# Second stick-breaking heads' queries and keys, and a third block of new rows, turned by DMA transposes

## The chip, the core and the metric

The kernel runs on one core of a Trainium2 chip. The metric is device time in microseconds (us) of one execution, lower is better. The engines of the core have queues of their own and run in order: TensorE (PE, with its weight loads as PEld), VectorE (DVE), ScalarE (ACT), GpSimd (POOL) and SyncE (SP), which here only issues DMAs.

## The reference, cut to what matters

One layer of a streaming encoder, 256 tokens, width 2048, all in float32. Eight "fox" heads (softmax attention with a forget bias) and eight stick-breaking heads, each 128 wide, stand side by side; a gated feed-forward network with a short convolution follows.

```
def stick_breaking_attention(q, k, v):
    scale = HEAD_DIM ** -0.5
        z = jnp.einsum('bhqd,bhkd->bhqk', qi.astype(jnp.float32), k32) * scale
        mask = k_pos[None, :] < q_pos[:, None]
        log_beta = jax.nn.log_sigmoid(z)
        log_one_minus = jnp.where(mask, log_beta - z, 0.0)
        suffix = lax.cumsum(log_one_minus, axis=key_axis, reverse=True) - log_one_minus
        weights = jnp.where(mask, jnp.exp(log_beta + suffix), 0.0)
        return jnp.einsum('bhqk,bhkd->bhqd', weights.astype(v.dtype), v)
...
        h = rms_norm(x, attn_norm[layer])
        x = x + hybrid_mixer(h, w_in[layer], ..., w_out[layer])
        h = rms_norm(x, ffn_norm[layer])
        x = x + conv_ffn(h, w_up[layer], conv_w[layer], conv_b[layer], w_down[layer])
```

## The kernel before

All weights are streamed once. A step loads 128x2048 float32 of weights by SP (`load`, L266; five buffers `w_raw`), ScalarE rounds them to `w_hi` (L276) and VectorE subtracts to get the rest, `w_lo` (L284); three products of high and low parts make one float32 product on PE. The Python loop at L1431 writes out the order of every engine by hand: in iteration n it emits the loads of step n+6, the cast and subtraction of step n+2, the matmuls of step n, what follows step n-1, and one or two "ticks" that move the attention heads on by a stage each (`tick`, L245). Each engine then works through its own list in that order.

Steps come in this order: the values of the fox heads, then "units" (L545) for rows rA and rB (queries and keys of the fox heads 0 to 3 and 4 to 7), rC (queries and keys of the stick-breaking heads 0 to 3), vB (their values), rD (queries and keys of stick-breaking heads 4 to 7), then the output projection, then the feed-forward network. The steps of the output projection are called W0 to W18 here. W0 to W10 take the fox heads: by `ORDER` (L1096) W1 and W3 make `acc_o` of the columns 2 (`out_rows(0, 2, ...)`), W5 and W9 those of columns 3, and the rest are products of `out_unit`, on the tiles `bank_a`, `bank_bc`, `bank_b`. W11 to W18 take the stick-breaking heads. W15 to W18 finish the columns c = 2 and c = 3, which are blocks 2 and 3 of the new rows.

A stick-breaking head (`sb_head`, L832) goes through: scores `ps_z` on PE (L840, L841), mask added by VectorE (L844), three activations of ScalarE on `e` (L847 to L849) and one VectorE operation on it (L850), high and low parts `sps` (L854, L855), sums with a triangular matrix on PE (L859, L861), weights `w` and their high and low parts `ws` (L864, L867 on ScalarE, L868 on VectorE), output `ps_o` on PE (L759, L761), eviction to `oSb`. Here the heads are numbered 0 to 7.

Queries and keys come out of a unit with tokens on partitions and must be turned so that the head's width is on partitions. For the fox heads and for rD this is done by PE (`to_heads`, L675: 16 transposes `ps_h` for rD, then four ScalarE evictions, the queries' with the scale 1/sqrt(128)). For rC it is done by DMA (`turned_heads`, L659): `send_turned` (L642) copies each 128x512 block to a tile `room`, its two 16-bit halves apart, the first block by ScalarE and the second by VectorE, and issues a DMA transpose on SP for each; three ticks later `take_turned` (L653) copies the halves back together. The scale of these queries is one VectorE operation (L672).

`heads_tile` (L350) has two buffers, which its callers take in turn: qB0, kB0, then kB1, qB1, so that kB1 stands where qB0 stood.

New rows x2 (tile `xb`) of 512 columns c are turned likewise for the feed-forward network: blocks c = 0 and 1 by DMA (`turned_rows`, L1002, then `split_turned`, L1017), c = 2 and 3 by PE (`next_rows`, L997: eight transposes `ps_x` each). The high and low parts go to `hT`. The first step of the feed-forward network reads blocks 0 and 1, its second step first block 2, then block 3 (L1229).

Of the kernel before, what the change touches and what calls it, by code (L numbers as in the profile page):

```python
# [9 lines left out]
F32 = mybir.dt.float32  # L10
# [6 lines left out]
P = 128  # L17
# [30 lines left out]
def hybrid_layer(  # L48
# [67 lines left out]
    rstd1 = const.tile([P, NT], F32, name="rstd1")  # L116
    headR = const.tile([P, NH], F32R, name="headR")
    nrstd1 = const.tile([P, NT], F32, name="nrstd1")
    hT = big.tile([P, KT, 2, S], F32R, name="hT")
    xp = xf.rearrange("(t p) d -> p t d", p=P)  # L120

# [416 lines left out]
    def of_sums(q):  # L538
        n, t = q
        return lambda i, p, _: sums_cell[1][:, p, n, i, t * P : (t + 1) * P]  # L540
# [1 line left out]
    def of_raw(kb, t):  # L542
        return lambda i, p, _: of_half(hT[:, 4 * kb + i], p, t)

    def unit(c_first, c_second, dst, done):  # L545

        cols = (c_first, c_second)
        w11, w12, w21, w22 = (rows_of(wi, 4 * h, 4, cols[n], 512) for h in range(2) for n in range(2))
        mem, bank = {}, {}
        slots = dict(zip("acbe", (0, 1, 2, 3) if turn[0] else (2, 3, 0, 1)))  # L550
        turn[0] ^= 1

        def r(t, negative=False):
            return (nrstd1 if negative else rstd1)[:, t : t + 1]

        def product(name, new, lhs, weights, load_=(), sums=None, plus=None, follow=None):
            parts = []

            def loads():
                for key, src in load_:  # L560
                    mem[key] = load(src)
                if plus is not None:
                    nc.gpsimd.dma_start(
                        mem[weights].rearrange("p (a b) -> p a b", a=4), plus, accum_op=ALU.add
                    )

            def prepare():
                parts.extend(split(mem[weights], 4, 512))

            def matmuls():  # L570
                if new:
                    bank[name] = bank_tile(f"bank_{name}", slots[name])
                in_three([bank[name]], parts, 4, lhs, new, True)

            new_step(loads, sums, prepare, matmuls, follow)

        def plain(n, kq, order, follow=None):
            def matmuls(parts):
# [12 lines left out]
        def sum_of(other):  # L591
            return lambda: dve.tensor_tensor(mem["11"], mem["11"], mem[other], op=ALU.add) and None

        out = {}

        def evict(name, n, t, negative=False):
            def follow():
                if not out:
                    out.update(dst())
                act.activation(out[n, t], bank[name], AF.Identity, scale=r(t, negative))  # L600
                yield

            return follow

        def add(name, n, t, negative=False):
            dve.scalar_tensor_tensor(
                out[n, t], bank[name], r(t, negative), out[n, t], op0=ALU.mult, op1=ALU.add
            )

        def then_add(*what):  # L610
            def follow():
                yield
                for w in what:
                    add(*w)

            return follow

        def finish():
            act.activation(out[0, 1], bank["a"], AF.Identity, scale=r(1))
            yield  # L620
            add("c", 0, 0)
            others.append(done(out))

        product("a", True, of_raw(0, 0), "11", [("11", w11)], follow=evict("a", 0, 0))
        product("c", True, of_raw(1, 0), "21", [("21", w21)])
        product("b", True, of_sums(T5), "11", [("12", w12)], sum_of("12"), follow=evict("b", 1, 1))
        plain(1, 0, [(1, "e"), (0, "b")])
        product("a", False, of_sums(S2), "11", [("22", w22)], sum_of("22"), follow=evict("a", 1, 0, True))
        plain(1, 1, [(1, "e"), (0, "b")], then_add(("e", 1, 1)))
        product("a", False, of_sums(T7), "12", plus=w22, follow=then_add(("a", 1, 1, True)))  # L630
        product("b", False, of_sums(S4), "22", follow=then_add(("b", 1, 0)))
        plain(0, 0, [(0, "c"), (1, "a")])
        product("a", False, of_raw(1, 1), "11", plus=w21)
        plain(0, 1, [(1, "a"), (0, "c")], finish)
# [4 lines left out]

        return make  # L640

    def send_turned(rows, room):  # L642
        planes = room.bitcast(U16).rearrange("p h s -> p (h s)").rearrange("p (t c) -> p t c", t=NT)
        for t, (move, (source, words)) in enumerate(zip((act.copy, dve.tensor_copy), rows)):
            move(
                planes[:, t].rearrange("p (b f) -> p b f", b=2),
                source.bitcast(U16).rearrange("p (f b) -> p b f", b=2),
            )
            nc.sync.dma_start_transpose(
                words.bitcast(U16).rearrange("p (g s) -> p g s", s=P), planes[:, t]  # L650
            )

    def take_turned(move, words, t, room):  # L653
        move(
            room.bitcast(U16).rearrange("p h (s b) -> p b h s", b=2)[:, :, :, t * P : (t + 1) * P],
            words.bitcast(U16).rearrange("p (b h s) -> p b h s", b=2, h=4),
        )

    def turned_heads(rows):  # L659
        for n, key in enumerate(("qB0", "kB0")):  # L660
            tile_of[key] = heads_tile(key)
            send_turned([(rows[n, t], rows[n, t]) for t in range(NT)], tile_of[key])
            yield
        yield
        yield
        yield
        for t in range(NT):
            take_turned(act.copy, rows[0, t], t, tile_of["qB0"])
        yield
        for t in range(NT):  # L670
            take_turned(dve.tensor_copy, rows[1, t], t, tile_of["kB0"])
        dve.tensor_scalar(tile_of["qB0"], tile_of["qB0"], QSCALE, None, op0=ALU.mult)  # L672
        yield

    def to_heads(rows, keys, scales):  # L675

# [12 lines left out]
    def fox_rows(half):  # L689
        def done(rows):  # L690
# [20 lines left out]
            yield from to_heads(rows, (f"qA{half}", f"kA{half}"), (gq, g_k))  # L711
            for h in range(4 * half, 4 * half + 4):
                waiting.append(fox_head(h, half))

        return done

    def sb_rows(half):
        def done(rows):
            if half:
                while started["sb"] < 4:  # L720
                    yield
                yield
                yield
                yield from to_heads(rows, ("qB1", "kB1"), (QSCALE, 1.0))
            else:
                while started["fox"] < NH:
                    yield
                yield from turned_heads(rows)
            ready.add(f"qB{half}")
            if "vB" in ready:  # L730
                start_sb(half)

        return done

# [156 lines left out]

    unit(0, WF, row_tiles("rA", 0), fox_rows(0))
    unit(512, WF + 512, row_tiles("rB", 1), fox_rows(1))
    unit(B0, B0 + WF, row_tiles("rC", 0), sb_rows(0))
    unit(B0 + 2 * WF, B0 + 2 * WF + 512, value_rows, values_done)
    D_UNIT = len(steps)
    unit(B0 + 512, B0 + WF + 512, row_tiles("rD", 0), sb_rows(1))
    W_OUT = len(steps)


# [99 lines left out]
        yield  # L1000

    def turned_rows(c):  # L1002
        if c == 0:
            room = heads_tile("xT0")
            w = at.tile([P, NT, 512], F32, name="xw0", tag="v0")
            words = [w[:, t] for t in range(NT)]
        else:
            room = at.tile([P, 4, S], F32, name="xT1", tag="v1")
            words = [rows_tile(f"xw1{t}", 1) for t in range(NT)]
        send_turned([(x2[:, t, c * 512 : (c + 1) * 512], words[t]) for t in range(NT)], room)  # L1010
        yield
        for t, move in enumerate((act.copy, dve.tensor_copy)):
            take_turned(move, words[t], t, room)
        following.append(split_turned(c, room))
        yield

    def split_turned(c, room):  # L1017
# [24 lines left out]
    def out_rows(group, c, kh):  # L1042
# [22 lines left out]
        def follow():  # L1065
# [8 lines left out]
            while group == 0 and held:  # L1074
                held.pop()()
            if group == 1:
                after.append(turned_rows(c) if c < 2 else next_rows(c))
                yield
                if c == 0:
                    spare.append(heads_tile("spare").rearrange("p a b -> p (a b)")[:, :512])  # L1080
# [319 lines left out]
    def factors1():  # L1400
        yield from token_factors(rstd1, ss1)
        dve.tensor_scalar(nrstd1, rstd1, -1.0, None, op0=ALU.mult)

    def head_parameters():
        columns(pcol, prow, 50)
# [95 lines left out]
```

## Time and profile before

| what | us |
|---|---|
| median of 3 runs (lowest, highest) | 1091.05 (1090.68, 1091.85) |
| the profiled execution, its own time | 1090.48 |
| its span, first to last instruction | 1088.7 |
| largest idle of ScalarE in the stretch of the change, before L915 | 4.47 |

The page cuts the span into 40 slices of 27.2 us; a digit is the busy share in tenths. ScalarE and VectorE read:

```profile
DVE  5988899889897877779978988889888889789996
ACT  6767797778766857667667777667667667677762
```

Counted from 0, the change lies in slices 10 to 14 (272 to 408 us). VectorE is close to full in slice 11 and has room in slice 12 and after; ScalarE has more room in slices 12 to 14. An average over a slice tells nothing of the order in which operations wait for each other, so the lists of instructions in order of time are needed.

### The profile page before, as it was taken

Reading aid. Unit: us, or ns where it says so; the run is one execution under the profiler, and the core shown is the slowest. Engines: PE = TensorE matmul, PEld = TensorE weight load, DVE = VectorE, ACT = ScalarE, POOL = GpSimd, SP = SyncE. Lnnn points to the kernel's source line nnn. Section 1 sums busy time; section 2 is a strip of 40 time slices with the busy share of each in tenths; the row PEclk is TensorE's granted clock in tenths of the full one; section 3 lists DMA queues with packets and bytes.
Section 4 is the critical chain, followed back from the end, with each engine's and each line's share of the span. In section 5 each row is a group of like instructions: output and inputs, shape, how many; then the busy total and the mean of one; then the engine's idle time right before and its main releaser. Section 6 shows DMA issues by size and latency. Waiting matters only on the chain.

```text
span 1088.7 us, 14642 instructions
## 1 busy us (share of the span) xinstructions
PE 1083.8 (100%) x5669; PEld 935.6 (86%) x5669; DVE 929.5 (85%) x927; ACT 761.5 (70%) x972; POOL 59.8 (5%) x53
## 2 busy tenths in 40 slices
PE   9999999999999999999999999999999999999998
PEld 9988888888888888888888888888888888888887
DVE  5988899889897877779978988889888889789996
ACT  6767797778766857667667777667667667677762
POOL 0000000001000000000000000100000000000000
PEclk9999999999999999999999999999999999999999
DMA  8897986989777765669899598996969699896995
GB/s 311 271 273 240 276 199 208 231 244 281 236 219 239 191 202 189 198 173 257 266 228 309 168 260 270 250 292 172 309 191 287 228 245 270 222 311 167 285 267 140
DMA packets 183663, 260.62 MB, mean 239 GB/s; under 512 B 13080, under 2 KB 106666, under 8 KB 183594
## 3 DMA queue, kind: packets, MB, share of 16 engines
q1 hardware_dynamic: 160138, 212.36, 57.9%
q0 software_dynamic: 23280, 47.19, 24.7%
q8 instruction: 44, 0.72, 0.3%
q14 instruction: 25, 0.20, 0.1%
q10 hardware_dynamic: 176, 0.14, 0.0%
HBM read 255.48 MB, written 2.10 MB: 237 GB/s over the span
## 4 chain that ended last, share of the span: by engine, by line
PE 100%; DVE 0%; issue 0%
PE pu L1235 45%; PE bank_a L304 18%; PE bank_b L304 11%; PE bank_c L304 6%; PE acc_o L304 6%; PE acc_v L424 4%; PE bank_e L304 3%; PE acc L304 2%; PE ps_x L194 1%; PE ps_o L759 1%; PE ps_h L683 0%; PE ps_z L840 0%; PE ps_o L761 0%; PE ps_i L188 0%; PE half L304 0%; PE ps_z L859 0%
## 5 line engine op out<-in xcount | busy, mean ns | idle before, releaser
L284 DVE TENSOR_TENSOR w_lo<-w_raw,w_hi 128x2048 fp32r<-128x2048 f32 (+2 forms) x251 | 555.8, 2218 | 120.4 <-ACT w_hi L276 119.4
L276 ACT CAST w_hi<-w_raw 128x2048 fp32r<-128x2048 f32 (+2 forms) x251 | 464.4, 1854 | 213.8 <-PE pu L1235 86.4
L1235 PE MATMUL pu<-hT,w_hi 128*128 128x512 f32 x1408 | 333.5, 389 | 0.0
L1235 PEld LDWEIGHTS pu<-hT,w_hi 128*128 128x128 f32 x1408 | 263.0, 188 | 53.7
L1235 PEld LDWEIGHTS pu<-hT,w_lo 128*128 128x128 f32 x1408 | 180.0, 191 | 6.6
L1235 PE MATMUL pu<-hT,w_lo 128*128 128x256 f32 x1408 | 182.0, 283 | 0.0
L1288 POOL DMA_DIRECT2D w_raw<-in_w_down_dram x31 | 39.8, 1302 | 712.9 <-DVE w_lo L284 386.9
L1160 ACT ACTIVATE tap<-up,ccol 128x256 f32<-128x256 f32 x176 | 74.6, 495 | 0.0
L304 PE MATMUL bank_a<-w_hi,hT 128*128 128x512 f32 x192 | 48.6, 395 | 0.0
L304 PEld LDWEIGHTS bank_a<-w_hi,hT 128*128 128x128 f32 x192 | 35.2, 188 | 6.8
L304 PE MATMUL bank_a<-w_hi,s 128*128 128x512 f32 x160 | 40.0, 392 | 0.0
L304 PE MATMUL bank_b<-w_hi,s 128*128 128x512 f32 x160 | 40.0, 392 | 0.0
L304 PE MATMUL bank_a<-w_hi,g 128*128 128x512 f32 x152 | 38.0, 392 | 0.0
L424 PE MATMUL acc_v<-w_hi,hT 128*128 128x344 f32 x192 | 35.7, 327 | 0.0
L304 PEld LDWEIGHTS bank_b<-w_hi,s 128*128 128x128 f32 x160 | 28.9, 189 | 5.3
L304 PEld LDWEIGHTS bank_a<-w_hi,s 128*128 128x128 f32 x160 | 28.9, 189 | 5.2
L1165 DVE TENSOR_TENSOR gate<-gate,tap 128x512 f32<-128x512 f32 x44 | 30.3, 689 | 2.3
L1165 DVE TENSOR_TENSOR val<-val,tap 128x512 f32<-128x512 f32 x44 | 30.3, 688 | 2.3
L1146 DVE TENSOR_TENSOR up<-t,R 128x512 f32<-128x512 f32 x44 | 30.5, 692 | 1.5
L304 PE MATMUL acc_o<-w_hi,oSb 128*128 128x512 f32 x128 | 31.7, 396 | 0.0
L1153 ACT ACTIVATE gate<-up,ccol 128x256 f32<-128x256 f32 x44 | 24.1, 594 | 10.8 <-DVE up L1146 5.4
L304 PEld LDWEIGHTS bank_a<-w_hi,g 128*128 128x128 f32 x152 | 27.4, 189 | 4.9
(304 smaller groups left out, 1420.1 us busy)
## 6 DMA issues: line engine op xcount, KB each, us to landing
w_raw<-in_w_up_dram SPq DMA_DIRECT2D x88, 1024.0 KB, 7.1
w_raw<-in_w_down_dram SPq DMA_DIRECT2D x44, 1024.0 KB, 6.9
w_raw<-in_w_in_dram SPq DMA_DIRECT2D x40, 1024.0 KB, 6.9
w_raw<-in_w_down_dram POOLq DMA_DIRECT2D x31, 1024.0 KB, 9.9
w_raw<-in_w_out_dram SPq DMA_DIRECT2D x16, 1024.0 KB, 6.5
w_raw<-in_w_in_dram POOLq DMA_DIRECT2D x10, 1024.0 KB, 9.8
w_raw<-in_w_in_dram SPq DMA_DIRECT2D x13, 516.0 KB, 5.1
xb<-in_x_dram POOLq DMA_DIRECT2D x4, 512.0 KB, 9.2
```

The lines of the kernel that those rows point to most:

```text
L194: nc.tensor.transpose(ps[:, j, t * P : (t + 1) * P], x2[:, t, (k + j) * P : (k + j + 1) * P], ident)
L276: copy(hi[:, :n], raw[:, :n])
L284: dve.tensor_tensor(lo[:, :n], raw[:, :n], f32(hi[:, :n]), op=ALU.subtract)
L304: nc.tensor.matmul(o, lhs(i, l, t), r[:, i, :] if cut is None else r[:, i, cut], start=starts and j == 0, stop=stops and j == 3 * n - 1, s ...
L424: nc.tensor.matmul(banks[j][t][:, :VC], of_half(hT[:, k], l, t), w[:, 0, m * VC : (m + 1) * VC], start=k == l == 0 and w is mem["parts", i ...
L759: mm(po, v, w[:, i, :S], start=m == 0, stop=False)
L1146: dve.tensor_tensor(u[:, :, 2:], t2, R, op=ALU.mult)
L1153: act.activation(a[:, j, :], u[:, j, 2:], AF.Identity, scale=ccol[:, 2, f : f + 1], bias=ccol[:, 3, f : f + 1],)
L1160: act.activation(taps[w][:, j, :], u[:, j, w : w + S], AF.Copy, scale=ccol[:, w, f : f + 1])
L1165: dve.tensor_tensor(a, a, tap, op=ALU.add)
L1235: nc.tensor.matmul(acc[:, j, S:] if low else acc[:, j, :], (lo if low else hi)[:, i, j * P : (j + 1) * P], hT[:, k, 0, :] if low else hT[: ...
L1288: nc.gpsimd.dma_start(mem[weights].rearrange("p (a b) -> p a b", a=4), plus, accum_op=ALU.add)
```

## The change

Unit rD's keys are sent by DMA as soon as head 3 has issued its scores (`second_keys`), and its queries when the unit is finished (`second_heads`); both are copied out and in by ScalarE alone. The start of the heads 4 to 7 is no longer behind `to_heads`. The queries' scale goes into the factors of the units rC and rD (`rstdq`), so L672 and the scale of the eviction go. Block c = 2 of the new rows is turned by DMA, and its split into high and low parts follows the take at once, in the same iteration, instead of with the next two iterations.

```
+    rstdq = const.tile([P, NT], F32, name="rstdq")
...
-    def unit(c_first, c_second, dst, done):
+    def unit(c_first, c_second, dst, done, factors=rstd1, keys=None):
...
+            return (nrstd1 if negative else rstd1 if n else factors)[:, t : t + 1]
...
-        product("b", False, of_sums(S4), "22", follow=then_add(("b", 1, 0)))
+        product("b", False, of_sums(S4), "22", follow=then_add(("b", 1, 0), then=keys))
...
+    def take_turned(words, room, moves=BOTH):
+        for t, (move, word) in enumerate(zip(moves, words)):
+            move(
+                room.bitcast(U16).rearrange("p h (s b) -> p b h s", b=2)[:, :, :, t * P : (t + 1) * P],
+                word.bitcast(U16).rearrange("p (b h s) -> p b h s", b=2, h=4),
+            )
...
+    def second_keys(rows):
+        while started["sb"] < 4:
+            yield
+        send_heads(rows, 1, "kB1", (act.copy, act.copy))
+        yield
+        yield
+        yield
+        take_heads(rows, 1, "kB1", act.copy)
+
+    def second_heads(rows):
+        send_heads(rows, 0, "qB1", (act.copy, act.copy))
+        yield
+        yield
+        yield
+        take_heads(rows, 0, "qB1", act.copy)
+        start_sb_when("qB1")
...
-    unit(B0 + 512, B0 + WF + 512, row_tiles("rD", 0), sb_rows(1))
+    unit(B0 + 512, B0 + WF + 512, row_tiles("rD", 0), second_heads, rstdq, second_keys)
...
+            room = at.tile([P, 4, S], F32, name="xT2", tag="v0")
+            words = [tmp.tile([P, 6 * P], F32, name=f"xw2{t}", tag="sps")[:, :512] for t in range(NT)]
         send_turned([(x2[:, t, c * 512 : (c + 1) * 512], words[t]) for t in range(NT)], room)
         yield
-        for t, move in enumerate((act.copy, dve.tensor_copy)):
-            take_turned(move, words[t], t, room)
-        following.append(split_turned(c, room))
+        take_turned(words, room)
+        if c == 2:
+            for _ in split_turned(c, room):
+                pass
+        else:
+            following.append(split_turned(c, room))
...
-                after.append(turned_rows(c) if c < 2 else next_rows(c))
+                after.append(turned_rows(c) if c < 3 else next_rows(c))
```

Three places show how the lists move. The first is ScalarE's list between head 2 and head 3. Before, behind head 2's weights and parts (the last row is the cast for W0):

```order
L864 ACTIVATE w<-ps_z 128x384
L867 CAST ws<-w 128x256
L854 CAST sps<-e 128x384
L974 CAST hT<-oFox 128x4x256
L276 CAST w_hi<-w_raw 128x2048
```

Now the two copies of the keys stand ahead of these casts:

```order
L880 ACTIVATE w<-ps_z 128x384
L883 CAST ws<-w 128x256
L870 CAST sps<-e 128x384
L650 COPY kB_2547<-rD_2281 128x1024
L650 COPY kB_2547<-rD_2282 128x1024
L990 CAST hT<-oFox 128x4x256
L277 CAST w_hi<-w_raw 128x2048
```

Further on in the same list, before, from the unit's last eviction (rD) over the casts for W2 and W3 to head 3's `w`:

```order
L619 ACTIVATE rD_2279<-bank_a,rstd_91 128x512
L276 CAST w_hi<-w_raw 128x2048 x2
L884 ACTIVATE oSb_2681<-ps_o,pcol 128x256
L768 ACTIVATE osq<-ps_o 128x256
L915 CAST hT<-oFox 128x2048
L864 ACTIVATE w<-ps_z 128x384
```

Now, with the takes of the keys ahead and the copies of the queries between the casts for W2 and W3:

```order
L660 COPY kB_2547<-rD_2281 128x2x4x128
L660 COPY kB_2547<-rD_2282 128x2x4x128
L622 ACTIVATE rD_2280<-bank_a,rstdq 128x512
L277 CAST w_hi<-w_raw 128x2048
L650 COPY qB_2667<-rD_2279 128x1024
L650 COPY qB_2667<-rD_2280 128x1024
L277 CAST w_hi<-w_raw 128x2048
L900 ACTIVATE oSb_2694<-ps_o,pcol 128x256
L784 ACTIVATE osq<-ps_o 128x256
L931 CAST hT<-oFox 128x2048
L880 ACTIVATE w<-ps_z 128x384
```

Six copies have come into this stretch, two of them (the takes of the queries) behind the last row shown.

The second place is VectorE's list at head 4's mask, before:

```order
L844 TENSOR_TENSOR ps_z<-ps_z,masksR 128x2x128
L1071 SCALAR_TENSOR_TENSOR xb<-acc_o_2667,rg_125,xb 128x512
L1071 SCALAR_TENSOR_TENSOR xb<-acc_o_2668,rg_125,xb 128x512
L284 TENSOR_TENSOR w_lo<-w_raw,w_hi 128x2048 x2
L850 SCALAR_TENSOR_TENSOR e<-ps_z,e 128x384
```

and now, where the operation on `e` stands right behind the mask (at head 5 too), and the rows' update and W5's and W6's subtractions behind it:

```order
L860 TENSOR_TENSOR ps_z<-ps_z,masksR 128x2x128
L866 SCALAR_TENSOR_TENSOR e<-ps_z,e 128x384
L1093 SCALAR_TENSOR_TENSOR xb<-acc_o_2680,rg_126,xb 128x512
L1093 SCALAR_TENSOR_TENSOR xb<-acc_o_2681,rg_126,xb 128x512
L285 TENSOR_TENSOR w_lo<-w_raw,w_hi 128x2048 x2
```

The heads 4 to 7 start half a step earlier on PE as well: head 4's output `ps_o` came after the first half of W9's matmuls and now comes ahead of them.

The third place is VectorE's list at the end of the output projection, before (`xb` in the last row but one is block 3's update):

```order
L205 SCALAR_TENSOR_TENSOR hT<-ps_x,pcol,hT 128x256 x2
L284 TENSOR_TENSOR w_lo<-w_raw,w_hi 128x2048
L205 SCALAR_TENSOR_TENSOR hT<-ps_x,pcol,hT 128x256 x2
L1120 MEMSET up_3426 128x2x2
L1120 MEMSET up_3427 128x2x2
L1071 SCALAR_TENSOR_TENSOR xb<-acc_o,rg_126,xb 128x512 x2
L284 TENSOR_TENSOR w_lo<-w_raw,w_hi 128x2048
```

and now, with a copy out, a take and four splits of block 2 ahead of block 3's update:

```order
L650 COPY xT_3355<-xb 128x1024
L285 TENSOR_TENSOR w_lo<-w_raw,w_hi 128x2048
L660 COPY xT_3355<-xw_3357 128x2x4x128
L1044 SCALAR_TENSOR_TENSOR hT<-xT_3355,pcol,hT 128x256 x4
L1142 MEMSET up_3414 128x2x2
L1142 MEMSET up_3415 128x2x2
L1093 SCALAR_TENSOR_TENSOR xb<-acc_o,rg_127,xb 128x512 x2
L285 TENSOR_TENSOR w_lo<-w_raw,w_hi 128x2048
```

More of the change, by code (lines that the diff above doesn't have):

```diff
@@ L551, in unit, with r @@
         turn[0] ^= 1
-        def r(t, negative=False):
-            return (nrstd1 if negative else rstd1)[:, t : t + 1]
+        def r(n, t, negative=False):
+            return (nrstd1 if negative else rstd1 if n else factors)[:, t : t + 1]
         def product(name, new, lhs, weights, load_=(), sums=None, plus=None, follow=None):
@@ L599, in follow @@
                     out.update(dst())
-                act.activation(out[n, t], bank[name], AF.Identity, scale=r(t, negative))
+                act.activation(out[n, t], bank[name], AF.Identity, scale=r(n, t, negative))
                 yield
@@ L606, in add, with then_add @@
             dve.scalar_tensor_tensor(
-                out[n, t], bank[name], r(t, negative), out[n, t], op0=ALU.mult, op1=ALU.add
+                out[n, t], bank[name], r(n, t, negative), out[n, t], op0=ALU.mult, op1=ALU.add
             )
-        def then_add(*what):
+        def then_add(*what, then=None):
             def follow():
@@ L614, in follow @@
                     add(*w)
+                if then is not None:
+                    others.append(then(out))
             return follow
         def finish():
-            act.activation(out[0, 1], bank["a"], AF.Identity, scale=r(1))
+            act.activation(out[0, 1], bank["a"], AF.Identity, scale=r(0, 1))
             yield
@@ L640, in row_tiles, with send_turned @@
         return make
-    def send_turned(rows, room):
+    BOTH = act.copy, dve.tensor_copy
+    def send_turned(rows, room, moves=BOTH):
         planes = room.bitcast(U16).rearrange("p h s -> p (h s)").rearrange("p (t c) -> p t c", t=NT)
-        for t, (move, (source, words)) in enumerate(zip((act.copy, dve.tensor_copy), rows)):
+        for t, (move, (source, words)) in enumerate(zip(moves, rows)):
             move(
@@ L651, in send_turned, with send_heads, take_heads, first_heads @@
             )
[L653 to L659, printed above, removed]
+    def take_turned(words, room, moves=BOTH):
[4 more added lines that the diff above has]
+            )
+    def send_heads(rows, n, key, moves=BOTH):
+        tile_of[key] = heads_tile(key)
+        send_turned([(rows[n, t], rows[n, t]) for t in range(NT)], tile_of[key], moves)
+    def take_heads(rows, n, key, move):
+        take_turned([rows[n, t] for t in range(NT)], tile_of[key], (move, move))
+    def first_heads(rows):
+        while started["fox"] < NH:
+            yield
         for n, key in enumerate(("qB0", "kB0")):
-            tile_of[key] = heads_tile(key)
-            send_turned([(rows[n, t], rows[n, t]) for t in range(NT)], tile_of[key])
+            send_heads(rows, n, key)
             yield
@@ L666, in turned_heads, with start_sb_when @@
         yield
-        for t in range(NT):
-            take_turned(act.copy, rows[0, t], t, tile_of["qB0"])
+        take_heads(rows, 0, "qB0", act.copy)
         yield
-        for t in range(NT):
-            take_turned(dve.tensor_copy, rows[1, t], t, tile_of["kB0"])
-        dve.tensor_scalar(tile_of["qB0"], tile_of["qB0"], QSCALE, None, op0=ALU.mult)
+        take_heads(rows, 1, "kB0", dve.tensor_copy)
         yield
+        start_sb_when("qB0")
+    def second_keys(rows):
[10 more added lines that the diff above has]
+        yield
+        yield
+        take_heads(rows, 0, "qB1", act.copy)
+        start_sb_when("qB1")
+    def start_sb_when(key):
+        ready.add(key)
+        if "vB" in ready:
+            start_sb(int(key[-1]))
     def to_heads(rows, keys, scales):
@@ L713, in done @@
                 waiting.append(fox_head(h, half))
[L715 to L731, printed above, removed]
         return done
@@ L893, in hybrid_layer @@
     unit(512, WF + 512, row_tiles("rB", 1), fox_rows(1))
-    unit(B0, B0 + WF, row_tiles("rC", 0), sb_rows(0))
+    unit(B0, B0 + WF, row_tiles("rC", 0), first_heads, rstdq)
     unit(B0 + 2 * WF, B0 + 2 * WF + 512, value_rows, values_done)
     D_UNIT = len(steps)
-    unit(B0 + 512, B0 + WF + 512, row_tiles("rD", 0), sb_rows(1))
+    unit(B0 + 512, B0 + WF + 512, row_tiles("rD", 0), second_heads, rstdq, second_keys)
     W_OUT = len(steps)
@@ L1002, in turned_rows @@
     def turned_rows(c):
-        if c == 0:
+        if c == 1:
+            room = at.tile([P, 4, S], F32, name="xT1", tag="v1")
+            words = [rows_tile(f"xw1{t}", 1) for t in range(NT)]
+        elif c == 0:
             room = heads_tile("xT0")
@@ L1007, in turned_rows @@
         else:
-            room = at.tile([P, 4, S], F32, name="xT1", tag="v1")
-            words = [rows_tile(f"xw1{t}", 1) for t in range(NT)]
+            room = at.tile([P, 4, S], F32, name="xT2", tag="v0")
+            words = [tmp.tile([P, 6 * P], F32, name=f"xw2{t}", tag="sps")[:, :512] for t in range(NT)]
         send_turned([(x2[:, t, c * 512 : (c + 1) * 512], words[t]) for t in range(NT)], room)
         yield
-        for t, move in enumerate((act.copy, dve.tensor_copy)):
-            take_turned(move, words[t], t, room)
-        following.append(split_turned(c, room))
+        take_turned(words, room)
[4 more added lines that the diff above has]
+            following.append(split_turned(c, room))
         yield
@@ L1402, in factors1 @@
         dve.tensor_scalar(nrstd1, rstd1, -1.0, None, op0=ALU.mult)
+        dve.tensor_scalar(rstdq, rstd1, QSCALE, None, op0=ALU.mult)
     def head_parameters():
```

## The prediction

> **What bounds the kernel now.** First the page: busy times and the chain that ended last.
>
> ```profile
> span 1088.7 us, 14642 instructions
> PE 1083.8 (100%) x5669; PEld 935.6 (86%) x5669; DVE 929.5 (85%) x927; ACT 761.5 (70%) x972; POOL 59.8 (5%) x53
> PE 100%; DVE 0%; issue 0%
> ```
>
> PE is busy throughout and is the whole chain. So each microsecond of work taken from PE is won, and each that PE is made to wait is lost for good, since no later slack gives it back. The profiled execution took 1090.48 us: 1.78 more than its span, 0.57 less than the median of the runs, 1091.05. The sums below are made against it.
>
> Second the chain in order of time (start, duration, what) where the change touches it:
>
> ```profile
> 292.78 0.87 PE ps_h L683 x8
> 293.65 2.75 PE bank_bc L304 x12
> 296.41 0.36 PE ps_o L759 x3
> 296.76 0.22 PE ps_o L761 x2
> 296.98 1.04 PE ps_h L683 x8
> ...
> 374.74 0.91 PE ps_x L194 x8
> ```
>
> **What goes.** 16 transposes of rD and eight of block 2: 0.87 + 1.04 + 0.91 = 2.82 us of PE. That is the whole prize, 0.26%. The scaling of the first queries (L672) goes from VectorE, beside a busy PE, so it wins nothing. The factor `rstdq` is one more 128x2 operation on VectorE, not in the trace; the nearest row takes 0.17, so it costs 0 to 0.17, and I take 0, since PE works on the values' products meanwhile.
>
> ```profile
> 295.95 0.17 DVE L990 TENSOR_SCALAR nrg<-rg 128x2 f32<-128x2 f32 x1
> ```
>
> What comes is copies and waits on ScalarE and VectorE. I follow their queues on the clock of before.
>
> **ScalarE falls behind.** Its list in order of time, with the idle time ahead of a row and its releaser in brackets:
>
> ```profile
> 211.97 1.05 ACT L645 COPY qB<-rC 128x1024 uint16<-128x1024 uint16 x1 [1.88 <-PE ps_s L788]
> ...
> 271.40 1.04 ACT L974 CAST hT<-oFox 128x1024 fp32r<-128x1024 f32 x1
> ...
> 282.09 1.92 ACT L276 CAST w_hi<-w_raw 128x2048 fp32r<-128x2048 f32 x1
> ...
> 291.95 1.91 ACT L915 CAST hT<-oFox 128x2048 fp32r<-128x2048 f32 x1 [4.47 <-DVE oFox L912]
> ```
>
> The keys' copies now stand where 271.40 starts. They write kB1, which lies where qB0 lay, so they wait for its last reader, head 3's scores in the chain:
>
> ```profile
> 273.35 0.22 PE ps_z L841 x2
> ```
>
> That is 273.57, a wait of 2.2 for which ScalarE had other work before. The first row above shows the same kind of wait at the first heads, 1.88, behind which PE lost nothing; so a wait here is no loss by itself, and what counts is which queue reaches PE late. Two copies of about 1.0 follow: ScalarE is 4.2 late, and behind it queue the casts for W0 and W1 and head 3's `e`. Short idle times take up some 1.2 of it, the keys' takes add 2.5 (two of 1.38, row further down): W2's cast starts at 287.6 instead of 282.09 and ends at 289.5.
>
> The queries' copies then wait for the last row of rD, which VectorE adds behind W2's subtraction:
>
> ```profile
> 287.65 0.74 DVE L606 SCALAR_TENSOR_TENSOR rD<-bank_c,rstd,rD 128x512 f32<-128x512 f32 x1
> ...
> 294.84 0.42 DVE L868 TENSOR_TENSOR ws<-w,ws 128x256 fp32r<-128x256 f32 x1
> ```
>
> Subtraction to 291.8 (2.3 behind the cast), rD's row to 292.5, copies to 294.5, W3's cast to 296.3, two evictions, and L915 starts at 296.9 instead of 291.95. The idle 4.47, the only cover for all this, is eaten, and ScalarE is 4.95 late. Head 3's `w` follows at 298.7; its `ws` on VectorE ends at 300.1 instead of 295.26. PE asked for it at 296.41, with 1.1 to spare; now it stands until 300.1. Here alone PE loses 300.1 - 296.5 and wins the second `ps_h`, 1.04: net 2.6 late, the first `ps_h` counted.
>
> **VectorE cannot catch up.** It is now about 5.0 late, and this stretch gives it no room (busy us of PE, PEld, DVE, ACT):
>
> ```profile
> 300.00:320.00 20.00, 20.00 (x93) 16.73 (x92) 19.84 (x19) 12.05 (x14) 1.29 (x1) 1.00 0.60 157
> ```
>
> Worse, at heads 4 and 5 the operation on `e` now follows the mask directly. Between them ScalarE needs three activations, each like
>
> ```profile
> 307.18 0.53 ACT L849 ACTIVATE e<-e 128x384 f32<-128x384 f32 x1
> ```
>
> so VectorE, which worked on subtractions meanwhile, stands still for 1.6 twice: 3.2. Against this, a subtraction (2.3) and a row update (0.7) that were ahead of head 4's `ws` come behind it. That `ws` is 5.0 + 3.2 - 3.0 = 5.2 late.
>
> **PE asks earlier.** Before, PE came to head 4's output after twelve matmuls of W9 and even then waited a little for `ws`:
>
> ```profile
> 322.43 2.75 PE acc_o L304 x12
> 325.18 0.55 PE ps_o L759 x3
> 325.73 0.22 PE ps_o L761 x2
> ```
>
> ```profile
> 325.22 0.30 PEld L759 LDWEIGHTS ps_o<-ws,vB 128*128 128x128 f32 x2 [0.24 <-DVE ws L868]
> ```
>
> So there was no slack. Now the output stands ahead of those twelve. PE is through with it at 325.95 + 5.2 = 331.15; with the same work done it stood at 325.95 - 2.75 = 323.2 before. It is 7.9 late, the 1.91 won counted in. Behind this place VectorE has room again (slice 12 of the page reads 7), and the heads 5 to 7 each find their `ws` early by the same count, so I add nothing; and nothing comes off, since PE has no idle time to give. The bounds of this term: if VectorE made good all that it was late, the 2.6 of head 3 would stay; if the subtraction and the update were still waited for, 3.0 more, 10.9.
>
> **SP's queue.** The keys' transposes stand ahead of W4's load and hold it until ScalarE's copies end, 275.6, and the two are issued (2.6, below):
>
> ```profile
> 270.51 0.37 SPq L270 DMA_DIRECT2D w_raw<-in_w_out_dram  x1
> ```
>
> The page has the median time from issue to landing of such a load:
>
> ```profile
> w_raw<-in_w_out_dram SPq DMA_DIRECT2D x16, 1024.0 KB, 6.5
> ```
>
> The load goes out 7.7 later, at 278.2, and lands near 285. Its first user, a VectorE sum behind rD's row, now starts at 292.4. It costs nothing, and would from 7 us more on.
>
> **Block 2.** A transpose pair, a take that waited for it, where the first copy will start, the end of block 3's update, its splits on VectorE, and PE's transposes of block 3:
>
> ```profile
> 365.39 2.62 SPq L649 DMA_TRANSPOSE xw<-xT  x2
> ...
> 370.03 1.38 ACT L654 COPY xT<-xw 128x1024 uint16<-128x1024 uint16 x1 [1.25 <-DMA xw<-xT]
> ...
> 376.66 0.82 ACT L202 ACTIVATE hT<-ps_x,pcol 128x256 fp32r<-128x256 f32 x2
> ...
> 382.99 0.74 DVE L1071 SCALAR_TENSOR_TENSOR xb<-acc_o,rg,xb 128x512 f32<-128x512 f32 x1
> ...
> 388.02 1.66 DVE L205 SCALAR_TENSOR_TENSOR hT<-ps_x,pcol,hT 128x256 fp32r<-128x256 f32 x4
> ```
>
> ```profile
> 386.68 0.87 PE ps_x L194 x8
> ```
>
> Copy 376.66 to 377.7; take 4.65 later (365.39 to 370.03), 382.3 to 383.7; four splits, VectorE's last at 385.9. Only then does VectorE update block 3, to 387.35 instead of 383.73. PE, 0.91 ahead, reaches `ps_x` at 385.8 and waits 1.5. Block 3's sums of squares, factors and splits follow its update and are 3.6 to 3.7 late as well: the splits start near 391.7, one each 0.42 (1.66 / 4). PE has done `ps_x` at 388.15, and block 2's matmuls, eight of 0.23 (2.75 / 12 in the chain) and eight of half that, at 391.0; then it wants a split every 0.23, the last at 391.7, and gets that at 393.4: 1.7 more. Net 1.5 + 1.7 - 0.91 = 2.3 lost.
>
> **Sum.** 1090.48 + 7.9 + 2.3 = 1100.7. Against the median of the runs the same difference would read 0.57 more, well inside the range.
>
> A rule of the Trainium skill bears on the trade: VectorE: DVE Perf Modes, section "Rules for kernel authors", says to turn 128x128 blocks on TensorE if PSUM may be the target, and its table of three paths gives 1309 ns by DMA for a block of 16-bit words. By that figure a transpose of eight blocks would be an estimated 10.5 us, and the keys' takes would hold ScalarE some 10 us longer; the pair that went from issue to take in 4.65 speaks against such a price, and for the direction.
>
> **Rivals.**
> - *Full gain.* Every copy fits ScalarE's idle time: 1090.48 - 2.82 = 1087.7. For it speaks ScalarE's 70%; the point that decides is head 3's `ws`, which may be 1.1 late and is 4.9 late by my count. It needs the kB1 wait and the wait for rD's row to be gone. 0.10.
> - *Block 2 alone.* The heads' waits are hidden, block 2's are not: -1.91 + 2.3, 1090.9. 0.10.
> - *Head 3 alone.* VectorE recovers behind it: 2.6 + 2.3, 1095.4. Against it speaks 19.84 of 20. 0.17.
> - *Late transposes.* They land as late as a weight load, 6.5 after the second's issue instead of some 3.3. The queries' have that room; block 2 does not and loses 3.2 more: 1103.9. The pair above, which took 4.65 in all, speaks against it. 0.05.
>
> **The numbers.** My forecast has 0.58. Slower by over 0.2% (about what a measurement of this kernel can tell from no change): 0.58 + 0.17 + 0.05 = 0.80; within: 0.10; faster: 0.10. The range leaves out the full gain alone, reaches down to block 2 alone and up to late transposes, which also holds half of the upper bound of the heads' term: 1090.5 to 1104. The forecast's own range, by the bounds of its two terms, is 1096 to 1104.
>
> **What would show it.** In the changed profile PE should idle for `ws` ahead of head 3's and head 4's `ps_o` (L775), some 4 and 2 us; ScalarE ahead of the first kB copy for head 3's scores (2.2) and of the first qB copy for rD's row (3); PE ahead of block 3's `ps_x` for the update (1.5). If PE stays at 100% there, I am wrong.

## The result and the profile after

The changed kernel takes 1102.89 us (median of 4 runs, 1102.51 to 1103.0), the kernel before 1090.97 beside it: ratio 1.011, 95% interval 1.0098 to 1.0122. It is 1.1% slower. The prediction said 1100.7 in a range of 1090.5 to 1104.

The profiled execution of the changed kernel took 1102.83 us; its span is 12.4 us longer than the one of before. The page, its busy times and the chain that ended last:

```profile
span 1101.1 us, 14612 instructions
PE 1086.1 (99%) x5645; PEld 935.1 (85%) x5645; DVE 931.0 (85%) x929; ACT 769.7 (70%) x978; POOL 59.3 (5%) x53
PE 93%; ACT 3%; DVE 2%; issue 1%; DMA 1%; SPq 0%; ACTq 0%; DVEq 0%
```

The chain that ended last, all PE before, now passes through ScalarE, VectorE and a DMA. What PE waited for between 265 and 420 us (engine, line, releaser: us in total, times, longest):

```profile
PE bank_a L305 <- ACT rD L622: 4.5, 1, 4.5
PE bank_a L305 <- ACT sps L870: 1.7, 1, 1.7
PE acc_o L305 <- DVE xb L1093: 1.6, 1, 1.6
PE ps_x L195 <- DVE xb L1093: 1.4, 2, 1.1
PE pu L1257 <- DVE hT L206: 1.0, 1, 1.0
```

In the kernel before, the same view has no row for PE. The sum is 10.2; that the forecast added 7.9 + 2.3 to the same figure is chance, since the forecast is net of the transposes saved and the waits are not. No row is for head 3's or head 4's `ps_o`, where the prediction looked for them.

How late PE is at the same work, from the start of the same row in the order of time of both traces:

| place on PE | before | after | late |
|---|---|---|---|
| head 2's output, ahead of the first new instruction's effect | 266.12 | 267.54 | 1.42 |
| the sums `pg`, behind W0 | 285.52 | 293.36 | 7.84 |
| W2 `bank_bc` (first `ps_h` gone) | 293.41 | 300.47 | 7.06 |
| W4 `bank_b` (second `ps_h` gone) | 303.90 | 309.90 | 6.00 |
| behind head 4's output and the twelve matmuls of W9 | 325.71 | 335.66 | 9.95 |
| block 3's `acc_o` (block 2's `ps_x` gone) | 375.41 | 384.41 | 9.00 |
| last matmuls on block 3's rows | 392.01 | 404.56 | 12.55 |

Behind that it stays so to the end. Three parts: 1.42 ahead of the change's place, 8.53 in the heads (9.95 - 1.42, net of the 16 transposes that they save), 2.60 at block 2 (12.55 - 9.95, net of eight transposes). The first wasn't foreseen at all.

**The heads.** ScalarE in order of time, with the idle time ahead of a row and its releaser:

```profile
275.03 2.00 ACT L650 COPY kB<-rD 128x1024 uint16<-128x1024 uint16 x2 [2.11 <-PE ps_z L857]
...
285.80 2.52 ACT L660 COPY kB<-rD 128x1024 uint16<-128x1024 uint16 x2
288.20 0.67 ACT L622 ACTIVATE rD<-bank_a,rstdq 128x512 f32<-128x512 f32 x1
288.77 1.89 ACT L277 CAST w_hi<-w_raw 128x2048 fp32r<-128x2048 f32 x1
293.68 2.00 ACT L650 COPY qB<-rD 128x1024 uint16<-128x1024 uint16 x2 [3.02 <-DVE rD L607]
...
298.02 1.91 ACT L931 CAST hT<-oFox 128x2048 fp32r<-128x2048 f32 x1
...
303.52 2.59 ACT L660 COPY qB<-rD 128x1024 uint16<-128x1024 uint16 x2 [0.62 <-DMA rD<-qB]
```

The two waits that the prediction named are there, 2.11 and 3.02. Between the keys' takes and W2's cast stands rD's last eviction, L622; it reads `bank_a`, and W0's product wants that bank. PE and the clock that it was granted (the last view's columns are busy us of PE, PEld, DVE, ACT, POOL, then the clock, DMA share, GB/s):

```profile
288.92 3.24 PE L305 MATMUL bank_a<-w_hi,hT 128*128 128x512 f32 x8 [4.54 <-ACT rD L622]
...
303.19 0.52 PE L775 MATMUL ps_o<-ws,vB 128*128 128x256 f32 x3
...
314.38 3.40 PE L305 MATMUL acc_o<-w_hi,hT 128*128 128x512 f32 x12 [1.60 <-DVE xb L1093]
...
329.54 2.06 PE L305 MATMUL bank_a<-w_hi,hT 128*128 128x512 f32 x8 [1.66 <-ACT sps L870]
```

```profile
289.00:290.00 1.00, 1.00 (x4) 0.81 (x5) 0.97 (x3) 1.00 (x1) 0.00 (x0) 0.79 1.03 401
290.00:291.00 1.00, 1.00 (x4) 0.81 (x3) 0.65 (x2) 0.66 (x1) 0.00 (x0) 0.50 0.79 307
...
292.00:293.00 1.00, 1.00 (x4) 0.80 (x3) 1.00 (x2) 0.00 (x0) 0.00 (x0) 0.50 0.00 0
293.00:294.00 1.00, 1.00 (x9) 0.92 (x8) 1.00 (x2) 0.32 (x1) 0.00 (x0) 1.00 0.00 0
```

The wait of 4.54 is followed by 3.4 us at half the clock: W0's twelve matmuls take 4.44 (288.92 to `pg` at 293.36) instead of 2.72 (282.80 to 285.52), another 1.7 at this place. Head 3's `ps_o` then finds its `ws`, ready at 301.2, without waiting. The other two waits, at `acc_o` and at W8's `bank_a`, follow VectorE's two idle times, one at each of the heads 4 and 5:

```profile
313.02 0.56 DVE L866 SCALAR_TENSOR_TENSOR e<-ps_z,e 128x384 f32<-128x384 f32 x1 [1.67 <-ACT e L865]
...
324.64 0.56 DVE L866 SCALAR_TENSOR_TENSOR e<-ps_z,e 128x384 f32<-128x384 f32 x1 [1.67 <-ACT e L865]
...
328.65 0.74 DVE L972 SCALAR_TENSOR_TENSOR xb<-bank_a,nrg,xb 128x512 f32<-128x512 f32 x1
```

The view names ScalarE's `sps` as what W8 waited for, but W8's product doesn't read `sps`. By the program it needs `bank_a` back from VectorE's L972, the last row, which ended at 329.39, 0.05 before `sps`.

**Block 2**, from the order of time on SP's queue, ScalarE, VectorE and PE:

```profile
387.61 2.62 SPq L654 DMA_TRANSPOSE xw<-xT  x2
...
392.25 1.39 ACT L660 COPY xT<-xw 128x1024 uint16<-128x1024 uint16 x1 [2.85 <-DMA xw<-xT]
...
396.50 0.74 DVE L1093 SCALAR_TENSOR_TENSOR xb<-acc_o,rg,xb 128x512 f32<-128x512 f32 x1
...
396.64 0.33 PE L195 MATMUL ps_x<-cs,xb 128*128 128x128 f32 x1 [1.09 <-DVE xb L1093]
397.30 0.99 PE L195 MATMUL ps_x<-cs,xb 128*128 128x128 f32 x7 [0.33 <-DVE xb L1093]
...
402.06 2.66 PE L1257 MATMUL pu<-hT,w_hi 128*128 128x512 f32 x8 [0.98 <-DVE hT L206]
```

PE waits 1.09 + 0.33 = 1.42 for block 3's update and 0.98 at its splits, and runs the eight matmuls there at the splits' pace, 2.66 instead of 2.00.

### The profile page after: what moved, and what is told of

Read it like the earlier page. It is cut to its first block, busy times and chain, and to the rows that moved or that the text cites. A ratio compares the mean times of both kernels' runs of the same rounds, so it can differ in the third digit from the quotient of the medians.

```text
span 1101.1 us, 14612 instructions
## 1 busy us (share of the span) xinstructions
PE 1086.1 (99%) x5645; PEld 935.1 (85%) x5645; DVE 931.0 (85%) x929; ACT 769.7 (70%) x978; POOL 59.3 (5%) x53
## 4 chain that ended last, share of the span: by engine, by line
PE 93%; ACT 3%; DVE 2%; issue 1%; DMA 1%; SPq 0%; ACTq 0%; DVEq 0%
PE pu L1257 44%; PE bank_a L305 18%; PE bank_b L305 10%; PE bank_c L305 6%; PE acc_v L425 4%; PE acc_o L305 3%; PE bank_e L305 2%; PE acc L305 2%; ACT w_hi L277 2%; DVE w_lo L285 1%; DMA xw<-xT 1%; PE ps_o L775 0%; PE ps_x L195 0%; PE ps_h L717 0%; DVE xb L1093 0%
```

## The experiments

Each was timed against the kernel before on the same chip (medians between 1090.3 and 1090.6 there); intervals are 95%.

**block2_only.** Before, with block 2's part of the change alone (its room and the splits at once as there):

```
-                after.append(turned_rows(c) if c < 2 else next_rows(c))
+                after.append(turned_rows(c) if c < 3 else next_rows(c))
```

> The kernel before with only its third block of new rows sent by DMA; the second heads stay on PE and there is no rstdq. My theory: the takes delay VectorE's update of block 3, PE waits 1.4 for it at ps_x and some 1.0 at the last splits, and 0.91 of transposes is saved: about +1.5 to +2.3 us against the kernel before (1092.5 to 1093.3). Rival: the two waits come only because the heads were already late; alone, block 2 wins its transposes, -0.9 (1090.1).

Measured 1092.7, ratio 1.0019 (1.001 to 1.0028): +2.15. The waits are the same without the heads, 1.03 + 0.33 at `ps_x` and 0.99 at the splits. So they are block 2's own, and the rival falls.

**shift_only.** Before, plus one line:

```
+    dve.memset(const.tile([P, NT], F32, name="unused"), 0.0)
```

> The kernel before with one unused 32-byte tile (and a memset of it) in place of rstdq, which moves hT and all weight tiles up by 32 bytes while the sums stay. My theory: in the changed kernel PE is 1.4 us late before the change's first new instruction, growing only at products whose stationary operand is a sum, because the weights now lie otherwise against the sums: +1.4 us (1092.4), and the sums' matmuls 398 ns instead of 393. Rival: the 1.4 us are a difference between two executions or of the factor itself: 0.

Measured 1092.05, ratio 1.0013 (1.0005 to 1.0022): +1.5. PE comes to head 2's output at 267.46, 1.34 later than before. In the built programs of the changed kernel and of this one `hT`, `w_hi` and `w_lo` lie 32 bytes higher than before (the first `w_hi` at 96704 instead of 96672), and `sums`, which is allotted from the other end, lies at 212896 in all three. The groups of matmuls on the sums (mean ns behind the busy time), of shift_only from 70 to 265 us, then of before:

```profile
L305 PE MATMUL bank_a<-w_hi,sums 128*128 128x512 f32 x74 | 19.1, 398 | 0.0
L305 PE MATMUL bank_b<-w_hi,sums 128*128 128x512 f32 x66 | 17.1, 399 | 0.0
```

```profile
L304 PE MATMUL bank_a<-w_hi,sums 128*128 128x512 f32 x73 | 18.5, 393 | 0.0
L304 PE MATMUL bank_b<-w_hi,sums 128*128 128x512 f32 x72 | 18.1, 393 | 0.0
```

Five units with four products on sums of twelve matmuls each are 240 matmuls; at 5 to 6 ns that is 1.2 to 1.4 us.

**no_shift.** The whole change, with the factor in a tile that is written only later:

```
-    rstdq = const.tile([P, NT], F32, name="rstdq")
+    rstdq = nrg0 = const.tile([P, NT], F32, name="nrg0")
...
-    nrg0 = const.tile([P, NT], F32, name="nrg0")
```

> The whole change, but rstdq lies in nrg0's tile, which is written only after rstdq's last use, so that no other tile moves. My theory: 1.4 us less than the changed kernel, 1101.5 (ratio to before about 1.0096). Rival (the address doesn't matter): 1102.9.

Measured 1101.54, ratio 1.0100 (1.0087 to 1.0114): 1.35 less than the changed kernel, or 0.9 less when each is taken against the kernel before beside it. The intervals of the two overlap, but the trace decides: PE comes to head 2's output at 266.05, where it was at 266.12 before and at 267.54 in the changed kernel. The 1.4 us are the tile's place, not its work. The experiments on the heads that follow start from this kernel.

**filler and filler18.** no_shift, with 36 or 18 matmuls of zeros ahead of W0's product:

```
-                in_three([bank[name]], parts, 4, lhs, new, True)
+                (idle(36) if first else None, in_three([bank[name]], parts, 4, lhs, new, True))
```

> The same as no_shift, and 36 matmuls of zeros (some 0.11 us each) on PE ahead of W0's product, where PE waits 4.5 us for ScalarE's eviction; nothing else moves. My theory: the long idle time halves PE's granted clock for about 3.4 us behind it (0.50 in the trace), which costs 1.7 us on top of the wait; with PE kept busy the clock stays at 1.00 and the time is 1.7 less than no_shift, 1099.8. Rival: the slow stretch behind the wait has another cause (late weights): same as no_shift; and if the zeros outlast the wait, more.

Measured 1102.26, ratio 1.0108 (1.0095 to 1.0122): not less. The 36 took 8.0 us and outlasted the wait by 3.0, but W0's twelve matmuls then took 2.86 (290.45 to 293.31) instead of 4.86 (287.44 to 292.30 in no_shift). So the slow stretch comes of PE's idle time, as the theory said, and not of late weights. The second kernel stays inside the wait:

> As filler, but 18 matmuls of zeros, which take half of the 8.0 us that the 36 took there, 4.0, and so end inside the 4.55 us wait at W0. In filler the zeros held W0 back by 3.0 us, but its twelve matmuls ran at a clock of 1.00 in 2.9 us instead of 4.9. My theory, costs that add up: 2.0 less than no_shift, 1099.6. Rival: behind W0 PE is held by VectorE and ScalarE anyway (head 4's scores, W8), so that what W0 loses is waited for there too: less than 0.7 won, 1100.9 to 1101.5.

Measured 1102.04, ratio 1.0105 (1.009 to 1.012): nothing won, which is the rival's side, and even above its 1101.5. PE was 2.1 earlier behind W0, and lost it at head 4's scores, where it waited 1.9 for the queries' take instead of 1.2, and where the clock now fell instead. PE's waits in this kernel:

```profile
PE ps_x L195 <- DVE xb L1093: 2.0, 2, 1.7
PE ps_z L856 <- ACT qB L660: 1.9, 1, 1.9
PE bank_a L305 <- ACT sps L870: 1.7, 1, 1.7
...
```

**late, start, late_start.** no_shift with the keys' take one tick later, with the heads' start one tick later, and with both:

```
         send_heads(rows, 1, "kB1", (act.copy, act.copy))
         yield
         yield
-        yield
+        yield; yield
         take_heads(rows, 1, "kB1", act.copy)
...
-        take_heads(rows, 0, "qB1", act.copy)
+        take_heads(rows, 0, "qB1", act.copy); yield
         start_sb_when("qB1")
```

> no_shift with the takes of the keys one tick later: on ScalarE alone, rD's last eviction and W1's cast now stand ahead of the two takes; no other engine's order changes. My theory, that ScalarE's queue makes the wait at W0: the eviction comes 2.5 us earlier, the wait falls from 4.55 to 2.0, too short for the clock to fall, and with costs that add up the time is 2.5 + 2.0 less than no_shift, 1097.0. Rival (what comes later holds PE anyway): 1100 to 1101.5.

> no_shift with heads 4 to 7 started one tick later, so that PE, VectorE and ScalarE have these heads in the order of the kernel before; the wait at W0 stays. My theory: the two idle times of VectorE (1.67 each) between mask and e go, and PE's waits at head 4's scores (1.2), at acc_o (0.2 and 0.4 of slower matmuls) and at W8 (1.7) with them: 3.5 less than no_shift, 1098.0. Rival: VectorE is late because of the takes and the copies, not of the heads' order, and PE finds the same lateness at another place: within 1 of no_shift.

> Both edits, late and start. If the costs add up and both theories hold: 1101.5 - 4.5 - 3.5 = 1093.5, of which block 2 is 2.2 above the kernel before, so the second heads' DMA would by itself cost some 0.8. If the later places hold PE anyway: no better than the better of late and start.

Measured: late 1100.86 (ratio 1.0093, 1.0079 to 1.0107), 0.7 less than no_shift; start 1097.5 (1.0065, 1.0052 to 1.0077), 4.0 less; late_start 1096.95 (1.0057, 1.0045 to 1.007), 4.6 less. In late, where the eviction and the cast for W2 go ahead of the takes, the wait at W0 fell from 4.55 to 2.16, about as expected, and PE was 4.7 earlier behind it. But all save about a microsecond was waited for again, so the rival holds:

```profile
PE ps_z L856 <- ACT qB L660: 2.3, 1, 2.3
PE bank_a L305 <- ACT rD L622: 2.2, 1, 2.2
PE bank_a L305 <- ACT sps L870: 1.7, 1, 1.7
...
PE ps_o L775 <- ACT ws L883: 1.0, 1, 1.0
```

In start VectorE's two idle times are gone, and with them PE's waits behind W0, at head 4's scores, `acc_o` and W8, as expected:

```profile
PE bank_a L305 <- ACT rD L622: 4.5, 1, 4.5
PE ps_x L195 <- DVE xb L1093: 1.3, 2, 1.0
PE pu L1257 <- DVE hT L206: 1.0, 1, 1.0
```

So the heads' order makes what comes behind W0, and the costs don't add up: a wait at W0 is partly cover for later ones. late_start is barely better than start, far from the 1093.5 of costs that add up. The clock's cost doesn't add up there either. Behind late_start's remaining W0 wait of 2.16 the clock fell in the profiled run, behind the same 2.16 in late it didn't (the stretch behind W0, late first, then late_start):

```profile
285.00:290.00 5.00, 5.00 (x27) 4.22 (x26) 4.97 (x8) 3.93 (x3) 0.00 (x0) 1.00 0.60 210
```

```profile
285.00:290.00 5.00, 5.00 (x19) 4.06 (x20) 4.97 (x8) 4.01 (x3) 0.00 (x0) 0.66 0.59 210
```

But of late_start's five runs the two whose mean clock was 1.000 took 1096.95 and 1097.53, no less than the three with 0.998 to 0.999 (1096.52 to 1096.99).

**spread and spread_q0.** The heads' part of the change alone. In spread the keys' copies come one tick later, which takes their takes to the place that they have in late, and the heads start as in start. In spread_q0 the queries' copies come a tick later too; that moves the start along, so start's own tick is left out:

```
         while started["sb"] < 4:
             yield
+        yield
         send_heads(rows, 1, "kB1", (act.copy, act.copy))
...
     def second_heads(rows):
+        yield
         send_heads(rows, 0, "qB1", (act.copy, act.copy))
```

> Second heads by DMA, block 2 on PE, rstdq in nrg0's tile. Against late_start the keys' copies come one tick later, behind W0's cast and head 3's e, so that ScalarE no longer stands 2.1 us for head 3's scores; the takes stay behind rD's last eviction and heads 4 to 7 start as before. late_start less block 2's 2.15 is 1094.8. My theory: the lateness of ScalarE's queue is the cause; W0's remaining wait (2.2) goes, and the 1.4 of matmuls at the halved clock behind it: 1091.2, no worse than the kernel before by more than 0.6. Rival: VectorE's stretch behind it holds PE whatever ScalarE does: 1094 to 1095.

> spread, and the queries' copies one tick later too (W2's cast and two evictions go ahead of them, so that ScalarE doesn't stand 2.5 us for rD's last row), with heads 4 to 7 still started at the tick of the kernel before. My theory: now no wait of ScalarE is left that PE feels, acc_o's wait for xb (1.0 and 0.3) goes, and most of the prize of 1.91 shows: 1088.7 to 1090, at or under the kernel before. Rival: the queries' transposes, which landed 7 to 8 us after the copies beside the weight loads, now come too late for head 4's scores, and PE waits there some 2 to 3: 1092 to 1094.

Measured: spread 1091.94 (1.0012, 1.0004 to 1.0021), spread_q0 1091.55 (1.0008, 0.9999 to 1.0017). The wait at W0 is gone in both, so ScalarE's queue was its cause, and the heads by DMA cost little. But they win nothing either: spread is slower than the kernel before by 1.4, with waits of 1.0 at head 3's `ps_o` and at `acc_o`, and spread_q0 by 1.0, which its interval doesn't tell from nothing. Both lie between what was expected and the rival's figure. In spread_q0 four small waits are left,

```profile
PE acc_o L305 <- DVE xb L1095: 0.7, 2, 0.5
PE ps_z L858 <- ACT qB L660: 0.3, 1, 0.3
PE ps_o L777 <- DVE ws L886: 0.2, 1, 0.2
PE ps_o L777 <- ACT ws L885: 0.2, 1, 0.2
```

and with the idle moments around them they eat the prize: from W2 (293.41 before, 293.45 here) to W5's second half (310.36 and 311.93) PE loses 1.53 although it saves 1.04 there.

**block2_early and block2_after.** block2_only with the copies of block 2 issued at once behind its update (the first half on VectorE; the transposes keep their place in SP's queue, for which the copies and the issues of the transposes are parted, not shown):

```
                 after.append(turned_rows(c) if c < 3 else next_rows(c))
+                if c == 2:
+                    next(after[-1])
...
```

> block2_only, but block 2's two copies are issued right behind its update, ahead of the squares on ScalarE and of W's subtraction on VectorE (the first half on VectorE); the DMA queue's order stays. My theory: the copies are done 1.9 us earlier, so is the take, block 3's update and its splits: PE's waits of 1.4 and 1.0 to 1.6 fall to 0 to 0.7 in all, and the time is 1090.0 to 1090.6, no slower than the kernel before. Rival: the take's own price on VectorE (0.78 and the wait for ScalarE's half, 1.15) holds the update all the same: above 1091.5.

and block2_only with block 3's update issued ahead of block 2's take, and no longer behind its splits (`update` holds the same two operations; where they stood they are left out):

```
         yield
+        if c == 2:
+            update(1, 3)
         for t, move in enumerate((act.copy, dve.tensor_copy)):
             take_turned(move, words[t], t, room)
```

> block2_only with one change of order, on VectorE alone: block 3's two updates stand ahead of block 2's take and splits, instead of behind them. My theory: VectorE's queue order makes the waits; the updates end near 383.7 as in the kernel before, PE's wait of 1.4 at block 3's ps_x goes, and of the 1.6 at block 3's last splits about half to all stays, since PE comes there 1.4 earlier and the splits only 1.3: 1091.0 to 1091.5, or 0.4 to 0.9 over the kernel before. Rival: VectorE's additional work is what counts, in whatever order: 1092.7 as block2_only.

Measured: 1093.65 (1.0027, 1.0017 to 1.0037) and 1094.34 (1.0032, 1.002 to 1.0045), where at most 1090.6 and 1091.5 were expected. All their runs but one lie above block2_only's 1092.05 to 1093.07. In block2_early ScalarE stood for the update with a weight's cast behind it, and VectorE's subtraction for the cast:

```profile
374.41 1.05 ACT L647 COPY xT<-xb 128x1024 uint16<-128x1024 uint16 x1 [1.87 <-DVE xb L1087]
...
377.31 2.29 DVE L285 TENSOR_TENSOR w_lo<-w_raw,w_hi 128x2048 fp32r<-128x2048 f32 x1 [2.33 <-ACT w_hi L277]
```

In block2_after PE's wait at `ps_x` went, as expected, and came back whole at the splits, 2.9 in one, with the clock at 0.50 behind it; the subtraction waited for the cast behind block 2's splits, which waited for the take, which waited for the DMA:

```profile
382.83 1.38 ACT L654 COPY xT<-xw 128x1024 uint16<-128x1024 uint16 x1 [2.85 <-DMA xw<-xT]
...
386.01 1.90 ACT L276 CAST w_hi<-w_raw 128x2048 fp32r<-128x2048 f32 x1
...
387.94 2.29 DVE L284 TENSOR_TENSOR w_lo<-w_raw,w_hi 128x2048 fp32r<-128x2048 f32 x1 [1.29 <-ACT w_hi L276]
...
392.80 3.76 PE L1247 MATMUL pu<-hT,w_hi 128*128 128x512 f32 x8 [2.93 <-DVE hT L205]
```

The clock goes with the rest: five of six runs, at a mean of 0.998, took 1094.0 to 1094.56, and the one at 1.000 took 1092.54, the rival's number. In block2_early it made no such difference: its two runs at 1.000, 1093.42 and 1093.7, lie among the other six (1093.19 to 1094.06), and the profiled one, whose clock fell behind `ps_x`, had no wait left at the splits. So VectorE's order decides only where PE stands; ScalarE, which waits for the DMA with a cast behind it, makes the lateness, as far as the trace of block2_after tells. That a faster landing would win the 0.91 wasn't tried. No version tried is faster than the kernel before.

## Why the prediction came out near, step by step

| term | predicted | changed kernel's trace | runs |
|---|---|---|---|
| `rstdq` | 0 (0 to 0.17) | 1.42 | 0.9 to 1.35 (no_shift), 1.5 (shift_only) |
| second heads, net | 7.9 | 8.5 | 8.4, by difference (11.9 - 1.35 - 2.15) |
| block 2, net | 2.3 | 2.6 | 2.15 (block2_only) |
| sum | 10.2 | 12.5 | 11.9 |

By the trace the sum fell 2.3 short, 1.4 of it the first term. That it stayed within the range is in part luck: the range reached up to 1104 for late transposes and for a slower VectorE, not for a moved tile.

- **PE is the bound, and what it waits is lost**: right; the lateness stays to the end. What the forecast doesn't say is that taking one wait away need not win its length: filler18 and late had PE 2.1 and 4.7 earlier behind W0 and won nothing and 0.7.
- **The prize, 2.82**: right; it shows in the first table as 0.78, 1.06 and 0.95 at the three places where transposes went.
- **`rstdq` costs at most 0.17**: the step that failed by size. It was priced as an instruction, 0 to 0.17; its cost, 1.42, is the 32 bytes by which it moved the weights against the sums. shift_only shows it without the factor.
- **ScalarE falls behind**: right in its times. With the 1.42 added, W2's cast was forecast for 289.0 and came at 288.77, the cast of the fox sums (L915, now L931) for 298.3 and came at 298.02, head 3's `ws` for 301.5 and ended at 301.2.
- **"Here alone PE loses 300.1 - 296.5"**: wrong in place and price. Behind the keys' takes I followed the casts and left out the eviction L622 among them, whose reader is W0's product. PE stood there for 4.54, took 1.7 more at half the clock, and so came to `ps_o` when `ws` was ready. That ScalarE's queue makes this wait is shown by late (2.2) and spread (none); that most of it would have been waited for later anyway, by filler18 and late.
- **VectorE stands still 1.6 twice, and PE asks earlier**: right; twice 1.67, and start, which undoes just that order, wins 4.0. PE's waits from it came at `acc_o` and W8, not at head 4's `ps_o`, but by then PE was as late as forecast: through that output at 332.84, forecast 331.15 + 1.42. The total held where the places didn't, because PE waits for the same late engines wherever it meets them first; filler18 and late show this for what PE lost at W0. That the 1.7 of slow clock, which the forecast didn't know of, left the total near the forecast is luck on the forecast's side: later waits swallowed it.
- **The queries' transposes have room**: wrong. Their second was issued at 296.1 and the take found it at 303.5, 7.4 later, where 3.3 was assumed. That delays head 4's scores (1.2 of wait in no_shift). So the rival of late transposes came true for the queries, with little effect, and not for block 2, where the pair again took 4.64 from issue to take.
- **Block 2**: right in mechanism. The wait for the update was 1.42 (forecast 1.5); that at the splits 0.98 and 0.66 of pace (forecast 1.7). What the forecast didn't see is that ScalarE, not only VectorE, holds the splits: block2_after.
- **SP's queue** with W4's load hidden: right; none of the waits above is for a load of weights.
- **The rivals**: full gain and block 2 alone needed heads without a wait that counts; head 3 alone needed VectorE to recover, and it stood still twice instead.

## What to carry to other kernels

When a copy or a take is put into an engine's queue, follow every instruction behind it to its reader, evictions above all, since what they free is a PSUM bank that PE may want at once. An engine that is idle 30% of the time isn't free: copies that had to wait for a release or a DMA cost their wait to everything behind them, and the heads' order and the copies' places were worth more (some 8 us between no_shift and spread_q0, block 2 left out) than the 1.9 that the heads were to save. A new small tile belongs in space that is already there, or its neighbours' addresses have to be compared before and after.

## What was not expected of the hardware

- **A wait can cost more than its length.** PE's granted clock fell to 0.50 for some 3.4 us behind waits of 4.54, 2.93 (block2_after), 2.32 (late, head 4's scores), 2.16 (late_start, W0) and 1.91 (filler18, head 4's scores), and in block2_early behind 1.74 and 0.33 close together; it didn't behind the 2.16 at W0 in late, the 1.70 and 0.33 in filler18, or any shorter one that was looked at. At W0 that was 1.7 us, which later waits swallowed; in block2_after, where nothing followed, it was 1.5 to 2.0 of the whole time, by the one run in which the mean clock stayed at 1.000. The Trainium skill, TensorE: Matmul & The Clock Gate, Part 1, describes half the clock after an idle window of about 3.4 us that runs freely, and full clock after a busy one. The length of the slow stretch agrees, and that like waits did and didn't bring it on fits a window that doesn't start with the wait; but waits shorter than that window brought it on here.
- **32 bytes were worth 1.4 us.** Matmuls whose stationary operand lies in `sums` took 398 ns instead of 393 when the weights lay 32 bytes higher. Why isn't shown. That the place does it and not the factor is: shift_only has the place alone, no_shift the factor alone.
- **One pair of DMA transposes landed later than another of the same size.** A pair took 4.64 from the first's issue to the take at block 2; the queries' pair took 7.4 from the second's issue alone. Weight loads were in flight beside the queries' (142 to 377 GB/s in the slices from 295 to 300, against 148 to 205 from 389 to 392 at block 2), but that they are the cause isn't shown.
